# A hybrid encoder block on one core: the third head pair's row-sum loads behind the fourth pair's keys' copy in SP's queue

## The chip, the cores and the metric

The kernel runs on one core of a Trainium2 chip. TensorE (PE) multiplies matrices into PSUM, VectorE (DVE) and ScalarE (ACT) work elementwise, GpSimd (POOL) does little here but issue some DMAs, and SyncE (SP) issues nearly all the DMAs. The metric is the device time of one execution in microseconds (us), the median of several runs; less is better.

## The reference

One encoder layer over 512 positions of width 1024, in float32. Cut to what matters:

```python
h = rms_norm(x, attn_norm_g)
xr, gate, q, k, v = split(h @ w_in)
y_rnn  = (rg_lru(conv(xr), forward) + rg_lru(conv(xr), backward)) * gelu(gate)
y_attn = dilated_attention(q, k, v, rel_bias)     # 8 heads of 64
x = x + concat(rms_norm(y_rnn), rms_norm(y_attn)) @ w_out
x = x + square(relu(rms_norm(x) @ w_up)) @ w_down
return rms_norm(x, final_norm_g)
```

In the attention, each of eight heads has three dilated windows of keys with a relative bias, whose results are combined by their softmax sums. Together they amount to one softmax over the keys, with the logarithm of how often a key occurs added to its bias: `softmax(q k^T / 8 + bias) v`. A softmax row is divided by its sum; these row sums are one of the things that the change moves.

## The kernel before

**Matmuls in three.** Every large product is made of float32 numbers split into a high and a low part, and takes three matmuls (lines 312 to 314: high times high, high times low, low times high). ScalarE makes the high part of a weight block (whi, line 247), DVE the low part (wlo, line 269). The raw block arrives from DRAM in one of three buffers of 128 x 1024 floats (wraw); once DVE has made the low part, the buffer is free and SP loads the next block into it (`emit_dma`, line 230).

**Attention in pairs of heads.** The eight heads are four pairs, i = 0 to 3, written out as a loop over i and over four steps u of each pair (from line 1142 on). All positions are sorted by parity, 256 even ones and then 256 odd ones. For a pair, PE computes scores of four query tiles, each against 416 keys (`att_s`, line 805): two tiles use keys 0 to 511 as they stand, the other two need the first half of the keys once more behind the second. DVE writes the split keys into kk (line 784), and SP then copies their first half behind them inside SBUF, 256 KB (line 785, `s_lo`). Each group of six matmuls (two heads, three products) writes two PSUM tiles. DVE adds the bias and takes a row minimum (line 821), ScalarE takes the exponentials and adds up each row (line 822), PE transposes the result (line 841), and PE multiplies it with the values (`att_av`, line 941, tile pav).

**Row sums.** When a pair's exponentials are done, `att_z` (at u = 2) takes reciprocals of its row sums on DVE and SP writes them, transposed, to DRAM (zd, 16 KB, line 873). `att_zd` has SP read them back in two loads of 128 KB, spread over the partitions (zrow, line 878). DVE multiplies pav with zrow when it empties pav's PSUM bank (yp, line 947), which happens at the start of the next pair, just before DVE takes up that pair's scores.

**PSUM.** Score tiles, pav, and the output projection's tiles (pwo) share a pool of four banks that go round in turn ("pj"). The second head's tile of the fourth group of scores gets the bank that pav had.

**The output projection beside the fourth pair.** Work on W_out is woven into the pairs as fillers, three matmuls at a time. From the second half of the third pair on it is the product of the recurrent half (pwo). The attention half of W_out is multiplied by a scheme with sums of blocks. `load_x` starts it: SP loads the residual rows (x, eight loads of 256 KB, line 1045) and three raw blocks of W_out ("12", "22", "21" into ws, 512 KB each, line 1048), and DVE forms sums of them (lines 1051 to 1062). `load_x` puts these into a list `more`, of which one entry is run at the end of each step u.

**What sets the order of issues.** PE, ScalarE, DVE and POOL run in the order in which the code is written. So does SP within the loop over pairs, except that the loads of W_up blocks that are written behind the loop are put by a scheduler where a buffer becomes free. SP's queue is strictly in order: an issue that has to wait for a semaphore holds all behind it.

Of the kernel before, what the change touches and what calls it, by code (L numbers as in the profile page):

```python
# [98 lines left out]
def hybrid_kernel(ctx: ExitStack, tc, xw0, xw, xn, w_in, w_v, w_out, w_up, w_dn, gates, vecs, bias, fg, out):  # L99
# [118 lines left out]
    def oblock(b):  # L218
        return w_out[1, int(b[1]) - 1, int(b[0]) - 1]
# [578 lines left out]
    def att_s(p):  # L798
        for u in range(4):
            qt = QSEQ[u]  # L800
            w = {(0, 0): TH + TH - WN, (0, 1): 0, (1, 0): TH - WN, (1, 1): TH}[QT[qt]]
            pss = psq[p, u] = [ps_("ps", ("pj", "gs", "et", "pj")[u]) for _ in range(2)]
            for i, (a, b) in enumerate(((0, 0), (0, 1), (1, 0))):
                for e, r in enumerate(halves):
                    nc.tensor.matmul(pss[e][:, :NK], lhsT=qs_[p, a][r, P * qt:P * qt + P], rhs=kks[p][r, b, w:w + NK], start=i == 0, stop=i == 2)  # L805

    def att_e(p, u):
        qt = QSEQ[u]
        par, far = QT[qt]
        v = int(par != far)  # L810
        if u == 0:
            en[2 * p], en[2 * p + 1] = {}, {}
            zs[p] = small("zz", 8)
        pss = psq.pop((p, u))
        c0 = (WN + P) * far
        for e in range(2):
            h = 2 * p + e
            t = g_("e")
            mn = small("mn", 1)
            x = t[:, :NK] if far else t[:, S - NK:]  # L820
            nc.vector.tensor_tensor_reduce(x, pss[e][:, :NK], tws[h, v][:, c0:c0 + NK], 1.0, 3.0e38, OP.add, OP.min, mn)
            act(x, x, AF.Exp, scale=-1.0, bias=mn, accum_out=zs[p][:, 4 * e + qt:4 * e + qt + 1])
            en[h][qt] = t
            if u in (1, 3):
                del tws[h, v]
        if u == 3:
            del qs_[p, 0], qs_[p, 1], kks[p]
# [39 lines left out]
    def att_z(p):  # L867
        rz, zt = [work.tile([P, 32], FT, name=n, tag="zt", bufs=3) for n in ("rz", "zt")]
        z = zs.pop(p)
        nc.vector.reciprocal(rz.rearrange("p (e r q) -> p e r q", e=2, r=4),  # L870
                             bass.AP(tensor=z.tensor, offset=z.offset, ap=[z.ap[0], [4, 2], [0, 4], [1, 4]]))
        nc.vector.transpose(zt, rz)
        nc.sync.dma_start(bass.AP(tensor=zd.tensor, offset=zd.offset + 32 * P * p, ap=[[32, 4], [P, 32], [1, 32]]), zt)

    def att_zd(p):
        zrow[p] = g_("zrow")
        for e in range(2):
            nc.sync.dma_start(zrow[p][halves[e]], bass.AP(tensor=zd.tensor, offset=zd.offset + 32 * P * p + 4 * S * e, ap=[[0, 16], [S, 4], [1, S]]))

    def att_y(p):  # L880
        y_add(1)
# [50 lines left out]
    def att_av(p, jts):  # L932
        if 0 in jts:
            pav[p] = ps_("pav", "gs" if p == 3 else "pj")
        for jt in jts:
            parts = av_parts(jt)
            for i, (ci, co) in enumerate(parts):
                for e in range(2):
                    a = slice(64 * e, 64 * e + 64)
                    h = 2 * p + e  # L940
                    nc.tensor.matmul(pav[p][a, co], lhsT=vs[:, jt, h * DH:(h + 1) * DH], rhs=et[h, jt][:, ci],  # L941
                                     start=jt == 0 and i == 0, stop=jt == 3 and i == len(parts) - 1, skip_group_check=True)
            for e in range(2):
                del et[2 * p + e, jt]
        if 3 in jts:
            y = g_("yp")
            nc.vector.tensor_tensor(y[:, ::-1], pav.pop(p), zrow.pop(p), op=OP.mult)
            yat[p] = y
            if p == 3:
                att_a(p)  # L950
                att_q(p)

    def att_q(p):
        y_sq(yat[p], 1)

    def att_a(p):
        at[p] = g_("at")
        act(at[p], yat[p], AF.Copy, scale=vec("yg", 4 + p))
# [56 lines left out]
    def fill(n):  # L1015
        for _ in range(n):
            if fillers and fillers[0] is None:
                fillers.popleft()
                load_x()
            if fillers:  # L1020
                fillers.popleft()()
# [6 lines left out]
    more = deque()  # L1028

    def add_x():  # L1030
        for fn in more.popleft() if more else ():
            fn()

    def load_x():
        xb = big.tile([P, KD, S], FT, name="x1", tag="bigA")
        ws = big.tile([P, 4, 1024], FT, name="ws", tag="bigB")
        b12, b22, b21, s1 = [ws[:, i, :] for i in range(4)]
        tt = nc.vector.tensor_tensor

        def chunk(n, t):  # L1040
            raws[C_WA + OSEQ.index(n)] = t

        def x_in(g, n):
            x1[g, n] = xb[:, 2 * g + n, :]
            return lambda: nc.sync.dma_start(x1[g, n], xn[2 * g + n])

        def w_in(t, b):
            return lambda: nc.sync.dma_start(t, oblock(b))

        def sum1():  # L1050
            tt(s1, b12, raws[C_WA], op=OP.add)

        def sum2():
            t = work.tile([P, 1024], FT, name="tw", tag="tw", bufs=4)
            tt(t, s1, b22, op=OP.add)
            chunk("s2", t)
            t4 = work.tile([P, 1024], FT, name="tw", tag="tw", bufs=4)
            chunk("s4", t4)
            more[1].append(lambda: tt(t4, t, b21, op=OP.add))

        def sum3():
            tt(b12, b12, b22, op=OP.add)

        for n, t in (("s3", b12), ("22", b22), ("21", b21), ("s1", s1)):
            chunk(n, t)
        x_in(0, 0)()
        x_in(1, 0)()
        more.append([w_in(b12, "12")])
        more.append([w_in(b22, "22")])
        more.append([sum1, x_in(2, 0), x_in(3, 0), w_in(b21, "21")])  # L1070
        more.append([sum2, x_in(0, 1)])
        more.append([sum3, x_in(1, 1)])
        more.append([x_in(2, 1), x_in(3, 1)])
        more.append([emit_dma])
        more.append([emit_dma])
        more.append([emit_dma])
# [39 lines left out]
    def beside(*key):  # L1116
        for e in plan.pop(key, ()):
            e()
# [15 lines left out]
    def turn(p, jt):  # L1134
        for e in range(2):
            att_t(2 * p + e, jt)

    def corner(p, jt):
        for e in range(2):
            att_c(2 * p + e, jt)  # L1140

    with tc.manual_schedule(engines={nc.sync.engine}):
        for i in range(4):
            for u in range(4):
                beside(i, u, -1)
                if u == 0:
                    if i:
                        att_av(i - 1, range(4))
                    att_s(i)
                    att_e(i, 0)  # L1150
                    att_e(i, 1)
                if u > 1:
                    turn(i, 2 * u - 4)
                if u == 2:
                    att_z(i)
                beside(i, u, 0)
                fill(1)
                if u > 1:
                    corner(i, 2 * u - 4)
                if u == (2 if i == 2 else 3):  # L1160
                    att_zd(i)
                if (i, u) == (3, 2):
                    act(warm, epsb, AF.Sqrt)
                beside(i, u, 1)
                fill(1)
                if u == 0:
                    att_e(i, 2)
                    att_e(i, 3)
                if u == 1 and 1 <= i < 3:
                    att_q(i - 1)  # L1170
                    att_a(i - 1)
                if u > 1:
                    turn(i, 2 * u - 3)
                    corner(i, 2 * u - 3)
                if u < 2 and i < 3:
                    for e in range(2):
                        load_tw(2 * (i + 1) + e, 1 - u)
                beside(i, u, 2)
                fill(1)
                if u == 3 and 1 <= i < 3:  # L1180
                    att_y(i - 1)
                beside(i, u, 3)
                fill(1)
                add_x()
                beside(i, u, 4)
# [650 lines left out]
```

## Time and profile before

| | |
|---|---|
| three runs | 525.31, 527.17, 527.94 us; median 527.17 |
| profiled execution | 525.55 us, with a span of 523.7 us from the first to the last instruction |
| PE busy | 515.4 us (98% of the span) |
| PE weight loads busy | 443.7 us (85%) |
| DVE busy | 430.5 us (82%) |
| ScalarE busy | 351.6 us (67%) |
| DMA moved | 105.15 MB, 201 GB/s in the mean |
| granted TensorE clock | 1.000 |

The four attention pairs take the span from about 90 to 175 us; the change lies between 142 and 155 us. In the rows of the views, a timeline row has the start and the duration in us, the engine, the line, the operation, out<-in, how many instructions are merged in it, and in brackets the idle time before it with what ended it. The duration of an SP row is that of issuing the DMA; when its data has landed is told by "DMA to landing" (from issue to landing) in the view of a tile. A row of the list of waits has who waited <- for whom, the time in all, how often, and the longest. A row of a window has its length, the busy time and number of instructions of PE, PE's weight loads, DVE, ScalarE and POOL, the granted clock, the busy share of the DMA engines, and GB/s.

### The profile page before, as it was taken

The page shows a single profiled execution, that of the slowest core. Times are in us where ns is not written, and L with a number is a line of the kernel's source. Part 1 is how long each engine was busy: PE and PEld are TensorE (multiplying, and loading weights), DVE is VectorE, ACT ScalarE, POOL GpSimd, SP SyncE. Part 2 cuts the span into 40 slices and gives each one's busy share as a digit, 9 for nine tenths or more (in the row PEclk, how much of TensorE's full clock was granted, in tenths as well). Part 3 has the DMA queues.
Part 4 walks back from the last instruction along what each step waited for, and adds up shares of the span by engine and source line. Part 5 has one row for each costly group of instructions (what it writes and reads, how often), then busy time and mean ns, then how long its engine had stood idle before and what let it go on. Part 6 is the DMA issues. An engine that isn't in the chain of part 4 may idle for free.

```text
span 523.7 us, 8226 instructions
## 1 busy us (share of the span) xinstructions
PE 515.4 (98%) x3021; PEld 443.7 (85%) x3021; DVE 430.5 (82%) x667; ACT 351.6 (67%) x571; POOL 66.1 (13%) x89
## 2 busy tenths in 40 slices
PE   9999999999989999999999999999999999999995
PEld 7857888877768788899999888888999999888884
DVE  6898995877869898898779987889765977986985
ACT  7579946749747758585578665566567677665655
POOL 0182000000010221001300312001101300131000
PEclk9999999999999999999999999999999999999999
DMA  7736645456585699947595899976987496799804
GB/s 288 237 85 194 163 145 180 120 177 173 138 293 189 171 202 239 357 135 197 133 228 132 220 273 278 310 273 161 280 262 183 113 222 208 160 285 257 204 1 161
DMA packets 40329, 105.15 MB, mean 201 GB/s; under 512 B 5056, under 2 KB 13376, under 8 KB 40288
## 3 DMA queue, kind: packets, MB, share of 16 engines
q1 hardware_dynamic: 32448, 78.07, 44.7%
q0 software_dynamic: 7696, 26.32, 27.3%
q8 instruction: 24, 0.39, 0.3%
q10 hardware_dynamic: 144, 0.23, 0.1%
q14 instruction: 17, 0.14, 0.1%
HBM read 95.59 MB, written 4.29 MB: 191 GB/s over the span
## 4 chain that ended last, share of the span: by engine, by line
PE 96%; DMA 2%; DVE 0%; ACT 0%; issue 0%; SPq 0%; DVEq 0%
PE pu L314 10%; PE pu L313 10%; PE pu L312 10%; PE pd L313 10%; PE pd L314 10%; PE pd L312 10%; PE pqk L312 3%; PE pqk L314 3%; PE pqk L313 3%; PE pwo L312 2%; PE pwo L313 2%; PE pwo L314 2%; PE pav L941 2%; PE ps L805 2%; PE pt L841 2%; PE pp L312 1%
## 5 line engine op out<-in xcount | busy, mean ns | idle before, releaser
L269 DVE TENSOR_TENSOR wlo<-wraw,whi 128x1024 fp32r<-128x1024 f32 x71 | 86.5, 1219 | 22.3 <-ACT whi L247 22.1
L247 ACT ACTIVATE whi<-wraw 128x1024 fp32r<-128x1024 f32 x67 | 70.8, 1058 | 37.9 <-PE pd L314 17.0
L312 PE MATMUL pd<-whi,ah 128*128 128x512 f32 (+1 forms) x195 | 75.3, 386 | 0.0
L313 PE MATMUL pd<-wlo,ah 128*128 128x512 f32 (+1 forms) x195 | 75.3, 386 | 0.0
L314 PE MATMUL pd<-whi,al 128*128 128x512 f32 (+1 forms) x195 | 75.2, 386 | 0.0
L314 PE MATMUL pu<-hh,wlo 128*128 128x256 f32 x224 | 63.4, 283 | 0.0
L313 PE MATMUL pu<-hl,whi 128*128 128x256 f32 x224 | 63.4, 283 | 0.0
L312 PE MATMUL pu<-hh,whi 128*128 128x256 f32 x224 | 63.4, 283 | 0.0
L312 PE MATMUL pu<-h2h,whi 128*128 128x256 f32 (+1 forms) x200 | 60.1, 301 | 0.0
L314 PE MATMUL pu<-h2h,wlo 128*128 128x256 f32 (+1 forms) x200 | 60.1, 300 | 0.0
L313 PE MATMUL pu<-h2l,whi 128*128 128x256 f32 (+1 forms) x200 | 60.0, 300 | 0.0
L269 DVE TENSOR_TENSOR wlo<-tw,whi 128x1024 fp32r<-128x1024 f32 x37 | 45.2, 1222 | 17.1 <-ACT whi L247 17.1
L247 ACT ACTIVATE whi<-tw 128x1024 fp32r<-128x1024 f32 x38 | 40.1, 1058 | 24.6 <-PE pd L314 6.1
L313 PEld LDWEIGHTS pu<-hl,whi 128*128 128x128 f32 x224 | 43.0, 192 | 0.0
L312 PEld LDWEIGHTS pu<-hh,whi 128*128 128x128 f32 x224 | 43.0, 192 | 0.0
L314 PEld LDWEIGHTS pu<-hh,wlo 128*128 128x128 f32 x224 | 43.0, 192 | 0.0
L312 PEld LDWEIGHTS pd<-whi,ah 128*128 128x128 f32 x195 | 36.6, 188 | 7.4
L314 PEld LDWEIGHTS pd<-whi,al 128*128 128x128 f32 x195 | 36.6, 188 | 7.3
L313 PEld LDWEIGHTS pd<-wlo,ah 128*128 128x128 f32 x195 | 36.6, 188 | 7.3
L247 ACT ACTIVATE whi<-ts 128x1024 fp32r<-128x1024 f32 x24 | 25.4, 1060 | 25.6 <-PE pd L314 17.8
L312 PEld LDWEIGHTS pu<-h2h,whi 128*128 128x128 f32 x200 | 38.3, 191 | 1.3
L313 PEld LDWEIGHTS pu<-h2l,whi 128*128 128x128 f32 x200 | 38.3, 191 | 1.3
(283 smaller groups left out, 1221.3 us busy)
## 6 DMA issues: line engine op xcount, KB each, us to landing
wraw<-in_w_up_dram SPq DMA_DIRECT2D x25, 512.0 KB, 4.1
ts<-in_w_dn_dram POOLq DMA_DIRECT2D x24, 512.0 KB, 13.2
wraw<-in_w_dn_dram SPq DMA_DIRECT2D x24, 512.0 KB, 10.3
tw<-in_w_up_dram SPq DMA_DIRECT2D x15, 512.0 KB, 6.9
tw<-in_w_up_dram POOLq DMA_DIRECT2D x15, 512.0 KB, 8.3
wraw<-in_w_in_dram SPq DMA_DIRECT2D x13, 512.0 KB, 3.6
ts<-in_w_dn_dram SPq DMA_DIRECT2D x8, 512.0 KB, 8.7
tw<-in_w_dn_dram SPq DMA_DIRECT2D x8, 512.0 KB, 4.8
```

Source lines behind the costliest of these rows:

```text
L247: act(hi, raws[i], AF.Copy)
L269: nc.vector.tensor_tensor(lo, r, f(splits[i][0]), op=OP.subtract)
L312: nc.tensor.matmul(o, lhsT=a[0], rhs=b[0], start=bool(first), stop=False, skip_group_check=on)
L313: nc.tensor.matmul(o, lhsT=a[0], rhs=b[1], start=False, stop=False, skip_group_check=on)
L314: nc.tensor.matmul(o, lhsT=a[1], rhs=b[0], start=False, stop=bool(last), skip_group_check=on)
L805: nc.tensor.matmul(pss[e][:, :NK], lhsT=qs_[p, a][r, P * qt:P * qt + P], rhs=kks[p][r, b, w:w + NK], start=i == 0, stop=i == 2)
L841: nc.tensor.transpose(pt[:, i * P:(i + 1) * P], en[h][qt][:, k:k + P], ident)
L941: nc.tensor.matmul(pav[p][a, co], lhsT=vs[:, jt, h * DH:(h + 1) * DH], rhs=et[h, jt][:, ci], start=jt == 0 and i == 0, stop=jt == 3 and i ...
```

## The change

Two edits, both to what SP issues in the third pair (i = 2). `att_zd(2)`, the two loads of the third pair's row sums, moves from step u = 2 to step u = 3, where the other pairs have it; there it stands behind the step's first work, which for the third pair holds the copy of the fourth pair's keys. And the first W_out block ("12"), which was loaded at the end of step u = 2, is loaded at the end of u = 3 together with the second ("22").

```diff
@@ load_x
         x_in(0, 0)()
         x_in(1, 0)()
-        more.append([w_in(b12, "12")])
-        more.append([w_in(b22, "22")])
+        more.append([])
+        more.append([w_in(b12, "12"), w_in(b22, "22")])
         more.append([sum1, x_in(2, 0), x_in(3, 0), w_in(b21, "21")])
@@ the loop over pairs i and steps u
                 beside(i, u, 0)
                 fill(1)
                 if u > 1:
                     corner(i, 2 * u - 4)
-                if u == (2 if i == 2 else 3):
+                if u == 3:
                     att_zd(i)
```

This is SP's queue in the third pair, steps u = 2 and u = 3, as the difference between the kernels. zrow are the row-sum loads, ws the W_out blocks, wraw a W_up block, kk the keys' copy, x the residual rows. A name in brackets is a counter that the issue waits for: the DMAHW ones count completed DMAs (eight of them, used in turn), the others instructions of an engine.

```order
 L1045 DMA x_1608<-in_xn_dram 128x512 [waits DMAHW0_49,PE_49]
 L1045 DMA x_1608<-in_xn_dram 128x512 [waits DMAHW1_49]
-L878 DMA zrow<-zd 64x1x512 [waits DMAHW7_49,DMAHW2_49]
-L878 DMA zrow<-zd 64x1x512 [waits DMAHW3_49]
-L1048 DMA ws<-in_w_out_dram 128x1024 [waits DMAHW4_49]
-L230 DMA wraw<-in_w_up_dram 128x1024 [waits DMAHW5_49,DVE_49]
-L785 DMA kk<-kk 128x2x256 [waits DMAHW6_49,DVE_49]
+L230 DMA wraw<-in_w_up_dram 128x1024 [waits DMAHW2_49,DVE_49]
+L785 DMA kk<-kk 128x2x256 [waits DMAHW3_49,DVE_49]
+L878 DMA zrow<-zd 64x1x512 [waits DMAHW7_49,DMAHW4_49]
+L878 DMA zrow<-zd 64x1x512 [waits DMAHW5_49]
+L1048 DMA ws<-in_w_out_dram 128x1024 [waits DMAHW6_49]
```

The two row-sum loads and the first W_out block, which stood ahead of the W_up block and the copy, now stand behind them. The loads still wait for the counter of the row sums' write to DRAM (DMAHW7); the copy waits for DVE alone.

This is PE in the changed kernel, in the fourth pair's scores, from the second group of six matmuls on. (The order of PE's instructions is the same in both.)

```order
L805 MATMUL ps<-kk,qh 128x416 x4
L805 MATMUL ps<-kk,ql 128x416 x2
L805 MATMUL ps<-kk,qh 128x416 [waits DMAHW3_49,PE_49]
L805 MATMUL ps<-kk,qh 128x416 [waits PE_49]
L805 MATMUL ps<-kk,qh 128x416 x2
L805 MATMUL ps<-kk,ql 128x416 x2
L805 MATMUL ps<-kk,qh 128x416 [waits DVE_49] x2
```

The third group's first matmul waits for the copy; it did so before, with another counter. The fourth group waits for DVE to have emptied its banks.

This is DVE's product that empties pav of the third pair:

```order
-L947 TENSOR_TENSOR yp<-pav,zrow 128x512 [waits DMAHW3_49,DMAHW2_49,PE_49]
+L947 TENSOR_TENSOR yp<-pav,zrow 128x512 [waits DMAHW5_49,DMAHW4_49,PE_49]
 L821 ISA e,mn<-ps,tw 128x416 [waits DMAHW7_49,DMAHW6_49,PE_49]
 L821 ISA mn 128x1
```

It stays where it was, in front of DVE's work on the fourth pair's scores, and waits for the two row-sum loads at their new place.

## The prediction

> **What bounds the kernel now.** I first read the page's busy times and the shares of the chain that ended last.
>
> ```profile
> PE 515.4 (98%) x3021; PEld 443.7 (85%) x3021; DVE 430.5 (82%) x667; ACT 351.6 (67%) x571; POOL 66.1 (13%) x89
> PE 96%; DMA 2%; DVE 0%; ACT 0%; issue 0%; SPq 0%; DVEq 0%
> ```
>
> TensorE sets the end: it is busy 98% of the span. The program's matmuls are not changed, so the only thing that this change can win or lose is time in which PE stands still. The second view is the list of PE's own waits over the whole span:
>
> ```profile
> PE ps L805 <- DMA kk<-kk: 2.1, 1, 2.1
> PE pwarm L142 <- PEq L1825: 0.8, 1, 0.8
> ```
>
> There are two rows, and the second is the start of the program. The first is one wait, for a DMA that copies a pair's key halves inside SBUF (kk<-kk). Third, the timeline of PE shows where. The first two rows are the third pair's scores and the matmul behind them, the others those of the fourth pair.
>
> ```profile
> 133.35 0.65 PE L805 MATMUL ps<-kk,qh 64*128 64x416 f32 x4
> 134.58 0.56 PE L805 MATMUL ps<-kk,qh 64*128 64x416 f32 x4
> 135.14 0.56 PE L805 MATMUL ps<-kk,qh 64*128 64x416 f32 x4
> 135.82 0.50 PE L312 MATMUL pqk<-h_hi,whi 128*128 128x512 f32 x1
> ...
> 152.61 0.65 PE L805 MATMUL ps<-kk,qh 64*128 64x416 f32 x4
> 156.08 0.65 PE L805 MATMUL ps<-kk,qh 64*128 64x416 f32 x4 [2.08 <-DMA kk<-kk]
> 157.40 0.51 PE L312 MATMUL pwo<-whi,yh 128*128 128x512 f32 x1
> ```
>
> A pair's scores are four groups of six matmuls. The first two use keys as DVE wrote them; the third and fourth read the copied half. In the third pair the four groups take 135.82 - 133.35 = 2.47 us, in the fourth 157.40 - 152.61 = 4.79 us. The difference of 2.32 us is what the late copy costs. It is a little more than the 2.08 us of the named wait, because the matmul stream also has to start again.
>
> Fourth, why the copy is late. These are SP's issues around it, its wait in this stretch, and the DVE rows that release them:
>
> ```profile
> 142.83 0.59 SPq L873 DMA_DIRECT2D zd<-zt  x1
> 143.51 1.19 SPq L1045 DMA_DIRECT2D x<-in_xn_dram  x2
> 148.62 1.18 SPq L878 DMA_DIRECT2D zrow<-zd  x2
> 149.85 0.57 SPq L1048 DMA_DIRECT2D ws<-in_w_out_dram  x1
> 150.52 0.38 SPq L230 DMA_DIRECT2D wraw<-in_w_up_dram  x1
> 151.00 0.65 SPq L785 DMA_DIRECT2D kk<-kk  x1
> SPq L878 <- DMA zd<-zt: 4.6, 2, 3.9
> 146.17 1.22 DVE L269 TENSOR_TENSOR wlo<-wraw,whi 128x1024 fp32r<-128x1024 f32 x1
> 147.31 0.69 DVE L784 TENSOR_TENSOR kk<-kraw,kk 128x512 fp32r<-128x512 f32 x1
> ```
>
> SP issues strictly in its order. It stood 3.9 us, from 144.70 to 148.62, in front of the third pair's row-sum loads (zrow<-zd), because the row sums had not yet landed in DRAM (zd<-zt, issued at 142.83). What the copy itself needs, the DVE subtraction at line 784, was done at 148.00. The copy went out at 151.00, 3.0 us later, only because of what stood ahead of it. It then moved behind 1.25 MB:
>
> ```profile
> 151.00 4.95 DMA kk<-kk
> DMA to landing us min/median/max: 2.5/2.6/5.0
> DMA to landing us min/median/max: 2.4/2.6/3.2
> ```
>
> The first row is from the chain of waits; the second gives all four pairs' copies, the third all eight row-sum loads, from issue to landing. The other three pairs' copies, with no large load right ahead, took about 2.6 us.
>
> **The change part by part.** No instruction is added or removed; five issues of SP change places.
>
> *The copy.* In its new place it is behind the two x loads and one W_up block (wraw). That block needs the buffer that line 269 frees at 146.17 + 1.22 = 147.39; its issue takes 0.38, so SP is free again at about 147.8. The copy then goes out when line 784 is done, at about 148.1: 2.9 us earlier. Landing is bounded by 2.5 us (an undisturbed copy) and 5.0 us (this one, with 1.25 MB ahead; now it is 0.5 MB and the rest of the x loads), so it lands between 150.6 and 153.1. PE wants it for the third group, at 152.61 + (134.58 - 133.35) = 153.84. Both ends are in time, by 0.7 us at the worst, so the wait goes wholly: **-2.32 us**. It would come back only with a landing of over 5.7 us.
>
> *The row sums.* They still can't go before zd has landed at about 148.6. They follow the copy's 0.65 us of issue and go at 148.75 and 149.35, only 0.13 us later than before. But they now have 0.75 MB ahead of them. Their reader is the DVE product yp<-pav,zrow, with what follows it:
>
> ```profile
> 152.75 0.69 DVE L947 TENSOR_TENSOR yp<-pav,zrow 128x512 f32<-128x512 f32 x1 [2.13 <-PE pav L941]
> 156.93 0.59 DVE L821 CUSTOM_DVE_ANT_0 e<-ps,tw 128x416 f32<-128x416 f32 x1 [1.32 <-PE ps L805]
> 158.98 1.22 DVE L1051 TENSOR_TENSOR ws<-ws,wraw 128x1024 f32<-128x1024 f32 x1
> 171.43 0.42 DVE L902 TENSOR_TENSOR ol<-at,oh 128x256 fp32r<-128x256 f32 x1 [1.28 <-ACT oh L897]
> DMA to landing us min/median/max: 4.7/4.7/4.7
> 143.51 5.58 DMA x<-in_xn_dram
> ```
>
> The last two rows are landings behind a full queue: the W_up block of 150.52 with 0.75 MB ahead (4.7 us, for its own 0.5 MB), and the first x load. So the second row-sum load lands between 149.35 + 2.5 = 151.85 and 149.35 + 5.6 = 154.95. I take 3.3 us: the block's 4.7 us less the 0.375 MB that a row-sum load is smaller, at the 288 GB/s that the queue moved from 150 to 154 us, which is the mean of these rows:
>
> ```profile
> 150.00:152.00 2.00, 2.00 (x22) 1.41 (x20) 0.62 (x1) 0.00 (x0) 0.00 (x0) 1.00 0.84 280
> 152.00:154.00 2.00, 2.00 (x16) 1.05 (x12) 1.22 (x4) 0.00 (x0) 0.00 (x0) 1.00 0.85 297
> 160.00:162.00 2.00, 2.00 (x10) 1.65 (x10) 1.72 (x3) 0.95 (x4) 0.00 (x0) 1.00 0.00 0
> ```
>
> That is 152.65, just before DVE starts yp today: **0**. The cover is the 2.13 us for which DVE waits on pav there. Gone, it costs this: yp frees the PSUM bank that the fourth group's second head writes, so PE loses time once yp ends after 152.61 + (135.14 - 133.35) = 154.40, that is once the sums land after 153.71. At 4.7 us of landing it is 0.34 us, at 5.6 us it is 1.24.
>
> *W_out's first block* goes out at about 150.0 instead of 149.85, the second at 150.6 instead of 151.7, the x loads and the third block about 1.1 us earlier. The reader of the first is DVE's sum at line 1051, now at 158.98. DVE loses its 1.32 us of idleness at 156.93 and gets there at 157.66, 7.6 us after the issue; a landing as late as the slowest of these blocks holds that sum, not PE: **0**. If that cover is gone too, DVE's 1.28 us of idleness at 171.43 takes up what it is late.
>
> *What is late next.* From 157.40 on PE has no wait in the whole list, so nothing new appears as long as its suppliers come 2.3 us earlier with it. The nearest is ScalarE's exponentials for the transposes:
>
> ```profile
> 163.00 0.82 PE L841 MATMUL pt<-ident,e 128*128 128x128 f32 x6
> 159.99 0.19 ACT L822 ACTIVATION_READ_ACCUMULATOR e<-e,mn 128x1 f32 x1
> 157.56 0.64 ACT L822 ACTIVATE e<-e,mn 128x416 f32<-128x416 f32 x1 [0.78 <-DVE mn L821]
> SPq L230 <- DVE wlo L269: 144.0, 41, 11.3
> ```
>
> They end at 160.18, and 0.78 us of that is a gap that the stall made, so they end at 159.4; the transposes move to 160.7, 1.3 us behind. The DMA rings are empty from 160 us (share 0.00 above), so no backlog is carried on. Later weight blocks are issued when DVE has split an earlier one (the last row: 41 times), so they are paced by the work and come earlier with it: **0**.
>
> Sum: -2.32 us. The profiled execution took 525.55 us (span 523.7), so it would take 523.2. It stands 1.6 us below the median of the three runs (527.17) and 0.24 above their lowest. From the median the same sum gives **524.9 us**.
>
> **The rivals.**
>
> *The row sums become the wait.* For it: they change from an empty queue to one with 0.75 MB ahead, and the rows with such a queue took 4.7 to 5.6 us. Against: they are small. With 5.6 us PE loses 1.24 us again and the gain is 1.1: 526.1 us. [...]
>
> *The copy isn't early: the change doesn't do what it says.* The chain of waits names the DVE product at line 982, not line 269, as what came before the W_up block's issue:
>
> ```profile
> 149.88 0.75 DVE x L982
> 150.63 0.27 SPq L230
> ```
>
> If the block really waited for that, it would still go at 150.6 and hold the copy till 151.0, as today. With 0.5 MB ahead instead of 1.25 the copy would land in time or nearly, but the row sums would go at 151.7 and 152.3 and, with the same 3.3 us, land at 155.6. yp would end at 156.3, PE's fourth group would start then and not at 156.73 as today, and the gain would be 0.4 us: 526.8. Against: SP's issues at 149.85 and 150.52 follow each other without a pause, and the buffer's last reader is line 269.
>
> *The gain is given back later.* 2.3 us is less than DVE's or a DMA chain's slack may be somewhere in the 360 us that follow; DVE is 82% busy. Against: PE's list of waits has no row there. No change: 527.2.
>
> *More than the sum.* The profiled execution is one of the quick ones. If the other runs are slower because this very copy is later in them, the change takes that too: 527.17 - 525.55 = 1.6 more, 523.3. Nothing in one trace tells.
>
> *Slower: the row sums so late that they cost more than the copy did.* PE's fourth group would have to start after 156.73, where it starts today; that is decided once the sums land after 156.0, 6.7 us after their issue. The slowest W_out block of this stretch took 8.7:
>
> ```profile
> 156.73 0.56 PE L805 MATMUL ps<-kk,qh 64*128 64x416 f32 x4
> DMA to landing us min/median/max: 5.3/7.0/8.7
> ```
>
> With 8.7 they land at 158.05, yp ends at 158.74, and PE is 2.0 us later than today: 529.2. Against: a block is four times as large as a row-sum load.
>
> **How the numbers follow.** Forecast 54%, row sums 12%, copy not early 7%, given back 11%, more 12%, slower 4%. A measurement of this kernel tells about 0.5%, 2.64 us, from no change. The forecast of 2.3 us lies just inside that bound; with medians of runs that spread over 2.6 us I give it four chances in nine to come out beyond, 24%, and with the 12% of "more" faster is 0.36. Slower by more than that is most of the last rival: 0.03. The rest, 0.61, is within. The range goes from 522.8 (the lowest run less the sum, and a little) to 527.3 (no gain).
>
> **What would show it.** In the profile after: PE's list of waits without the row of kk<-kk; 2.5 us from the fourth pair's first score matmul to the pwo matmul behind it; SP's copy at about 148.1, ahead of the row sums at 148.8; yp at line 947 still released by PE pav and not by a DMA. If yp is released by zrow, the first rival holds; if SP's W_up block still goes at 150.6, the second; if a new PE wait of 1 to 2 us stands after 160 us, the third. A trace that has all the steps right and a time that hasn't moved would make the prediction wrong in its last step only.

## The result

The changed kernel took 524.34 us in the median of nine executions, the kernel before 527.40 us: a ratio of 0.995 with a 95% interval of 0.9929 to 0.9971. Three of all executions stand outside every comparison, because TensorE was much slower in them than in the others: the profiled one of the changed kernel (1044.51 us; its large matmuls took 670 ns in the mean instead of 386, though its granted clock is listed as 1.000), one of the kernel before (735.14, mean granted clock 0.656) and one of an experiment (861.35, 0.558). The profile shown here is from a repetition of the changed kernel (first experiment below), whose profiled execution took 523.33 us with a span of 521.5.

The page's busy times and PE's list of waits, of the changed kernel:

```profile
PE 515.0 (99%) x3021; PEld 443.6 (85%) x3021; DVE 430.1 (82%) x667; ACT 351.1 (67%) x571; POOL 66.2 (13%) x89
PE pwarm L142 <- PEq L1825: 0.8, 1, 0.8
PE pxr L453 <- ACT w3h L357: 0.2, 1, 0.2
```

The wait for kk<-kk is gone, and nothing has come in its place; both rows are from the first 5 us of the program. SP's issues, PE's fourth score groups and DVE's reader of the row sums, from the timeline of the changed kernel:

```profile
143.02 0.59 SPq L873 DMA_DIRECT2D zd<-zt  x1
143.70 1.28 SPq L1045 DMA_DIRECT2D x<-in_xn_dram  x2
147.60 0.33 SPq L230 DMA_DIRECT2D wraw<-in_w_up_dram  x1
148.21 0.65 SPq L785 DMA_DIRECT2D kk<-kk  x1
148.95 1.20 SPq L878 DMA_DIRECT2D zrow<-zd  x2
150.21 1.08 SPq L1048 DMA_DIRECT2D ws<-in_w_out_dram  x2
...
152.80 0.65 PE L805 MATMUL ps<-kk,qh 64*128 64x416 f32 x4
154.03 0.55 PE L805 MATMUL ps<-kk,qh 64*128 64x416 f32 x4
154.59 0.56 PE L805 MATMUL ps<-kk,qh 64*128 64x416 f32 x4
155.26 0.50 PE L312 MATMUL pwo<-whi,yh 128*128 128x512 f32 x1
...
153.72 0.69 DVE L947 TENSOR_TENSOR yp<-pav,zrow 128x512 f32<-128x512 f32 x1 [2.56 <-PE ps L805]
DMA to landing us min/median/max: 4.0/4.0/4.0
```

The copy goes at 148.21 instead of 151.00, right after DVE has made the keys. The four score groups take 155.26 - 152.80 = 2.46 us, as in the third pair, instead of the 4.79 of before. But yp starts 0.9 us after the first score matmul, though pav is done by then: it now waits for the row sums, whose second load went at about 149.6 and took 4.0 us (last row, issue to landing). The bracket of the yp row names PE's score matmuls, whose results yp doesn't read; in a later profile of the same kernel (last experiment) it names the load:

```profile
153.86 0.69 DVE L947 TENSOR_TENSOR yp<-pav,zrow 128x512 f32<-128x512 f32 x1 [2.43 <-DMA zrow<-zd]
```

PE does not notice: neither profile has a wait for yp.

### The profile page after: what moved, and what is told of

Same layout as the page of the kernel before. It is cut to its first block, busy times and chain, and to the rows that moved or that the text cites. A ratio compares the mean times of both kernels' runs of the same rounds, so it can differ in the third digit from the quotient of the medians.

```text
span 1042.7 us, 8224 instructions
## 1 busy us (share of the span) xinstructions
PE 1036.4 (99%) x3021; PEld 754.3 (72%) x3021; DVE 441.6 (42%) x667; ACT 356.6 (34%) x571; POOL 61.4 (6%) x89
## 4 chain that ended last, share of the span: by engine, by line
PE 99%; ACT 0%; DVE 0%; issue 0%
PE pu L313 10%; PE pu L314 10%; PE pu L312 10%; PE pd L312 10%; PE pd L313 10%; PE pd L314 10%; PE pqk L312 3%; PE pqk L313 3%; PE pqk L314 3%; PE pwo L314 3%; PE pwo L313 3%; PE pwo L312 3%; PE pav L941 2%; PE pt L841 2%; PE ps L805 2%; PE pg L528 1%
## 5 line engine op out<-in xcount | busy, mean ns | idle before, releaser
L312 PE MATMUL pd<-whi,ah 128*128 128x512 f32 (+1 forms) x195 | 130.6, 670 | 0.0
L313 PE MATMUL pd<-wlo,ah 128*128 128x512 f32 (+1 forms) x195 | 130.6, 670 | 0.0
L314 PE MATMUL pd<-whi,al 128*128 128x512 f32 (+1 forms) x195 | 130.3, 668 | 0.0
L313 PE MATMUL pu<-hl,whi 128*128 128x256 f32 x224 | 99.0, 442 | 0.0
L314 PE MATMUL pu<-h2h,wlo 128*128 128x256 f32 (+1 forms) x200 | 95.9, 480 | 0.0
L312 PE MATMUL pu<-h2h,whi 128*128 128x256 f32 (+1 forms) x200 | 95.7, 478 | 0.0
L314 PEld LDWEIGHTS pu<-hh,wlo 128*128 128x128 f32 x224 | 79.1, 353 | 0.0
L313 PEld LDWEIGHTS pu<-hl,whi 128*128 128x128 f32 x224 | 78.3, 349 | 0.2 <-issue 0.2
L312 PEld LDWEIGHTS pu<-hh,whi 128*128 128x128 f32 x224 | 77.7, 347 | 0.2 <-issue 0.2
L314 PEld LDWEIGHTS pu<-h2h,wlo 128*128 128x128 f32 x200 | 67.1, 336 | 5.2 <-issue 4.8
```

Of the source, the lines that this page charges most:

```text
L312: nc.tensor.matmul(o, lhsT=a[0], rhs=b[0], start=bool(first), stop=False, skip_group_check=on)
L313: nc.tensor.matmul(o, lhsT=a[0], rhs=b[1], start=False, stop=False, skip_group_check=on)
L314: nc.tensor.matmul(o, lhsT=a[1], rhs=b[0], start=False, stop=bool(last), skip_group_check=on)
```

## The experiments

All were timed against the kernel before on the same chip. This table splits each profiled span at two marks of PE: the fourth pair's first score matmul, and the first pwo matmul behind the scores. The last two columns are PE's named wait in the scores, in this one profiled execution, and how many of all executions had a mean granted clock of 0.996 or less. (For the kernel before these are its executions beside all the experiments; the row of the copy issued by ScalarE takes two runs together.)

| kernel | to the scores | scores | to the end | PE's wait | low clock |
|---|---|---|---|---|---|
| before | 152.61 | 4.79 | 366.3 | 2.08, kk | 36 of 79 |
| before, second profile | 152.84 | 4.40 | 367.9 | 1.68, kk | (among them) |
| changed | 152.80 | 2.46 | 366.2 | none | 0 of 30 |
| only the row sums moved | 152.57 | 3.68 | 366.2 | 0.58, yp | 0 of 12 |
| only the W_out block moved | 153.37 | 3.01 | 366.2 | 0.28, kk | 0 of 11 |
| row sums behind all | 153.58 | 6.43 | 367.8 | 3.52, yp | 7 of 7 |
| copy issued by ScalarE | 152.73 | 2.47 | 366.2 | none | 1 of 18 |
| copy behind all | 152.86 | 8.05 | 368.1 | 4.27, kk | 6 of 6 |

### The changed kernel again

No edit.

> The changed kernel once more, unchanged, because its one profile so far shows PE at about half its speed for the whole run (PE busy 1036.4 us) and can't be read against the profile of before. Theory (the late keys' copy was the only PE wait, and it goes): the copy is issued near 148.1 us and lands before 153.8; PE's list of waits has no kk<-kk row; from the fourth pair's first score matmul to the pwo matmul behind it 2.5 us instead of 4.79; yp at line 947 still follows PE pav; span 521.2 to 522.5; 2.3 to 3.0 us faster than the kernel before. First rival (row sums become the wait): yp is released by a DMA, and up to 1.2 us of PE wait stands in the fourth score group. Second rival (the copy isn't early): the W_up block is still issued near 150.6.

Measured: 523.93 against 526.25 us, ratio 0.9951 (0.9931 to 0.9971). The first theory holds in all but one point: yp no longer follows PE pav. That is the first rival's sign, but its PE wait isn't there. The second rival falls: the W_up block went at 147.60.

### The kernel before again

No edit.

> The kernel before once more, unchanged, for a second profile of it and as a measure of what no change looks like. Its nine runs spread over 4.2 us (524.83 to 529.01), those of the changed kernel over 1.1 us (523.95 to 525.00). Theory with the rival of more gain than the sum: the extra time of the longer runs is the same copy landing still later, so in this profile the PE wait for kk<-kk differs from 2.08 us by about as much as the run's time differs from 525.55, within 0.5 us. Against it: the wait is again 2.1 us within 0.3 while the time is another, so the spread comes from elsewhere. Timed: a ratio of 1.000 within 0.002.

Measured: 527.18 us, ratio 1.0007 (0.9979 to 1.0034). The profiled execution took 526.91 us, 1.36 more than the first one, and yet its wait for the copy is shorter. The list of waits, the copy's issue, the landing of all four pairs' copies, and a table of stretches of 2 us (the third last column is the granted clock):

```profile
PE ps L805 <- DMA kk<-kk: 1.7, 1, 1.7
149.63 0.65 SPq L785 DMA_DIRECT2D kk<-kk  x1
DMA to landing us min/median/max: 2.5/2.6/6.1
154.00:156.00 2.00, 0.33 (x6) 0.12 (x3) 1.84 (x8) 1.60 (x5) 0.00 (x0) 1.00 1.03 409
156.00:158.00 2.00, 2.00 (x14) 1.62 (x15) 1.25 (x5) 1.62 (x6) 0.00 (x0) 0.82 1.03 405
158.00:160.00 2.00, 2.00 (x7) 1.52 (x6) 2.00 (x5) 2.00 (x9) 0.00 (x0) 0.50 0.40 146
160.00:162.00 2.00, 2.00 (x9) 1.63 (x8) 0.13 (x2) 0.61 (x1) 0.00 (x0) 0.82 0.00 0
162.00:164.00 2.00, 2.00 (x11) 1.64 (x10) 2.00 (x3) 0.73 (x1) 0.00 (x0) 1.00 0.00 0
```

So this longer execution is not one in which the copy landed still later; that reading falls. The copy even went 1.37 us earlier than in the first profile, but, with the same 1.25 MB ahead, took 6.1 us to land instead of 4.95, so the wait is only 0.4 us shorter: the time of issue alone doesn't set it. What comes instead is in the clock. Behind the wait, TensorE is granted half its clock (0.50 from 158 to 160 us). The clock lacks 0.36 + 1.00 + 0.36 = 1.72 us of these 6, which is 3.4 us at one half. The first profile of the kernel before, and that of the changed kernel, have 1.00 in this whole stretch. From the first pwo matmul to the first transpose behind it PE took 164.43 - 157.24 = 7.19 us, against 163.00 - 157.40 = 5.60 in the first profile: the drop cost 1.6 us.

```profile
157.24 0.78 PE L312 MATMUL pwo<-whi,yh 128*128 128x512 f32 x1
164.43 0.82 PE L841 MATMUL pt<-ident,e 128*128 128x128 f32 x6
```

The other executions have no profile, but their mean clocks and times go together. The 43 executions of the kernel before with a mean clock above 0.996 have a median of 525.55 us, its 36 others one of 527.94. Seven of the 36 stand apart, with 0.991 and a median of 529.78; no profile shows why.

### One half: only the row sums move

```diff
-                if u == (2 if i == 2 else 3):
+                if u == 3:
                     att_zd(i)
```

> One half of the change: only the third pair's row-sum loads move behind the keys' copy; the first W_out block stays ahead, at the end of step u = 2, and is issued near 144.8 us because SP no longer stands there for the row sums. Theory (SP's wait in front of the row-sum loads, not the W_out block's bytes, made the copy late): the copy goes at about 148.1 with 1 MB ahead, lands 152 to 153.1, before PE's third group at 153.84: the whole gain, within 0.5 us of the changed kernel. Rival (bytes ahead count as much): the copy lands after 153.84 and PE keeps a wait of 0.5 to 1.5 us.

Measured: 524.58 us, ratio 0.9970 (0.9955 to 0.9986), 0.65 us more than the changed kernel. That is just outside the 0.5 us of the theory. The copy was in time or nearly, as the theory has it (PE's list has no wait for it, and the third group came 1.37 us behind the first, against 1.23 in the changed kernel): SP's wait in front of the row-sum loads (3.9 us in the first profile of the kernel before) had made it late. But the gain isn't whole, for a reason that neither theory named. PE's list of waits, PE's fourth group and yp:

```profile
PE ps L805 <- DVE yp L947: 0.6, 1, 0.6
155.50 0.64 PE L805 MATMUL ps<-kk,qh 64*128 64x416 f32 x3 [0.58 <-DVE yp L947]
154.75 0.69 DVE L947 TENSOR_TENSOR yp<-pav,zrow 128x512 f32<-128x512 f32 x1 [4.27 <-PE ps L805]
DMA to landing us min/median/max: 5.3/5.5/5.7
```

With the W_out block ahead as well, the two row-sum loads took 5.3 and 5.7 us to land (last row), yp ended at 155.4, and the fourth group's second head had to wait for it. Moving the W_out block too takes this wait away.

### The other half: only the W_out block moves

```diff
-        more.append([w_in(b12, "12")])
-        more.append([w_in(b22, "22")])
+        more.append([])
+        more.append([w_in(b12, "12"), w_in(b22, "22")])
```

> The other half: only the first W_out block moves behind the copy; the row-sum loads stay in front and hold SP until the row sums have landed, at about 148.6. Theory: the copy goes at about 150.3 with 0.75 MB ahead and lands 154.2 to 155.0, so a PE wait of 0.4 to 1.2 us for kk<-kk is left, and the gain is 1.1 to 1.9 us. Rival (bytes ahead count, not SP's wait): the wait is gone and the whole gain of 2.3 us is there. Rival (neither half does anything alone): no gain.

Measured: 524.50 us, ratio 0.9970 (0.9955 to 0.9986).

```profile
149.06 1.18 SPq L878 DMA_DIRECT2D zrow<-zd  x2
150.96 0.64 SPq L785 DMA_DIRECT2D kk<-kk  x1
155.05 0.65 PE L805 MATMUL ps<-kk,qh 64*128 64x416 f32 x4 [0.28 <-DMA kk<-kk]
DMA to landing us min/median/max: 3.9/3.9/3.9
```

Counted back from the first score matmul, the copy goes 153.37 - 150.96 = 2.41 us ahead instead of 152.61 - 151.00 = 1.61, and with 0.5 MB less ahead of it it landed in 3.9 us instead of 4.95 (last row). Together that is 1.85 us, and a wait of 0.28 us is left, less than the 0.4 to 1.2 that was expected. So taking away the block's issue and bytes removes most of the wait, just as taking away SP's stand for the row sums did in the other half: either cure is nearly enough for the copy. Each half is worth some 1.7 us, and the two together not the sum, since there is only one wait to remove.

### The row sums further back

The changed kernel, with the row-sum loads behind both W_out blocks.

```diff
-                if u == 3:
+                if u == 3 and i != 2:
                     att_zd(i)
...
                 add_x()
+                if (i, u) == (2, 3):
+                    att_zd(i)
```

> The changed kernel, but the third pair's row-sum loads go still further back, behind both W_out blocks: 1.75 MB ahead of them instead of 0.75. Theory (yp frees the PSUM bank of the fourth score group, so row sums that land after about 153.8 cost PE one for one): they landed 4.0 us after issue with 0.75 MB ahead; with 1 MB more at 290 to 380 GB/s they land at about 156.4 to 157.2, yp ends near 157.5, and PE waits 2.3 to 3.2 us in the fourth group for yp: the gain is gone, 526 to 527.5 without a drop of the clock. Rival (DVE's idleness hides it): no PE wait, the time of the changed kernel, 523.9.

Measured: 529.54 us, ratio 1.0050 (1.0021 to 1.0079): slower than the kernel before.

```profile
PE ps L805 <- DVE yp L947: 3.5, 1, 3.5
158.50 0.69 DVE L947 TENSOR_TENSOR yp<-pav,zrow 128x512 f32<-128x512 f32 x1 [6.48 <-DMA zrow<-zd]
159.25 0.46 PE L805 MATMUL ps<-kk,qh 64*128 64x416 f32 x2 [3.52 <-DVE yp L947]
160.00:162.00 2.00, 2.00 (x7) 1.55 (x7) 2.00 (x9) 2.00 (x7) 0.00 (x0) 0.61 0.07 23
162.00:164.00 2.00, 2.00 (x7) 1.57 (x6) 2.00 (x7) 2.00 (x7) 0.00 (x0) 0.53 0.00 0
```

The theory's chain is there: late row sums, late yp, PE's fourth group waiting for the PSUM bank. The size expected was too small (3.52 us came, not 2.3 to 3.2), and here too the clock falls to one half behind the wait, for (0.78 + 0.94) / 0.5 = 3.4 us. All seven executions have a mean clock of 0.995 or less.

### The copy from another queue

The kernel before, with the fourth pair's copy issued by ScalarE.

```diff
-            nc.sync.dma_start(f(k[:, :, S:]), f(k[:, :, :TH]))
+            (nc.scalar if p == 3 else nc.sync).dma_start(f(k[:, :, S:]), f(k[:, :, :TH]))
```

> The kernel before with one thing changed: the fourth pair's keys' copy is issued from ScalarE's queue instead of SP's, so it waits for DVE's subtraction alone while the row-sum loads stay in front in SP's queue (the W_up block then falls behind the W_out blocks in SP's queue). Theory (only the place in SP's queue made the copy late): it goes near 148.2, lands by 151.5, PE has no wait for kk<-kk nor for yp, and the time is that of the changed kernel within 0.5 us, 523.4 to 524.4. Rival (the gain of the change comes from the W_out and x loads that go earlier with it): these stay where they were, so no gain, 526 to 527.

Measured: 523.48 us, ratio 0.9947 (0.9925 to 0.9969). The whole gain, with the row sums where they were before.

```profile
148.89 0.68 ACTq L785 DMA_DIRECT2D kk<-kk  x1
148.84 1.18 SPq L878 DMA_DIRECT2D zrow<-zd  x2
152.73 0.65 PE L805 MATMUL ps<-kk,qh 64*128 64x416 f32 x4
155.20 0.50 PE L312 MATMUL pwo<-whi,yh 128*128 128x512 f32 x1
```

Only the copy's place mattered for the wait: the row sums and the first W_out block kept theirs in SP's queue, and the score groups take 2.47 us. The rival isn't tested as cleanly as was meant, because with the copy and the W_up block out of their way the second W_out block and the x loads went earlier here too (x at 151.19 instead of 152.34). Against it stands that PE's list of before has no wait for any of these loads, and that the span behind the scores is the same in both kernels, 366.2 and 366.3 us. One of the 18 executions of this version has the lower mean clock (0.994, 527.42 us); it has no profile, so its cause is open.

### The wait made longer

The kernel before, with the copy behind all three W_out blocks.

```diff
-            nc.sync.dma_start(f(k[:, :, S:]), f(k[:, :, :TH]))
+            if p < 3:
+                nc.sync.dma_start(f(k[:, :, S:]), f(k[:, :, :TH]))
...
-        more.append([w_in(b22, "22")])
-        more.append([sum1, x_in(2, 0), x_in(3, 0), w_in(b21, "21")])
+        more.append([w_in(b22, "22"), w_in(b21, "21")])
+        more.append([sum1, x_in(2, 0), x_in(3, 0)])
...
                 add_x()
+                if (i, u) == (2, 3):
+                    nc.sync.dma_start(f(kks[3][:, :, S:]), f(kks[3][:, :, :TH]))
```

> The kernel before with its one PE wait made about twice as long: the keys' copy goes behind all three W_out blocks (1.75 MB ahead, issued near 151.8). The last profile of the kernel before showed the granted clock at one half for some 3.3 us right behind the wait, 1.6 us lost, and the profile of the first did not. Theory (the wait itself may drop the clock, and the longer it is the more often): PE wait 3.3 to 4.3 us; nearly every execution has a mean clock of 0.996 or less; time 529 to 531, that is the wait's extra 1.7 and a drop in nearly all runs. Rival (the drop comes from elsewhere and has nothing to do with the wait): the same share of runs at a low clock as the kernel before has (20 of 45), and 527.5 to 528.5.

Measured: 530.40 us, ratio 1.0068 (1.0043 to 1.0092). (Line 805 is line 806 here.)

```profile
PE ps L806 <- DMA kk<-kk: 4.3, 1, 4.3
156.00:158.00 2.00, 0.00 (x0) 0.00 (x0) 0.00 (x0) 1.03 (x4) 0.00 (x0) 1.00 1.05 394
158.00:160.00 2.00, 1.47 (x8) 1.50 (x10) 0.06 (x1) 0.00 (x0) 0.00 (x0) 0.50 1.04 403
160.00:162.00 2.00, 2.00 (x9) 1.31 (x8) 2.00 (x7) 1.43 (x5) 0.00 (x0) 0.50 0.15 57
162.00:164.00 2.00, 2.00 (x6) 1.58 (x5) 1.23 (x3) 1.79 (x5) 0.00 (x0) 0.50 0.00 0
164.00:166.00 2.00, 2.00 (x8) 1.60 (x7) 0.22 (x1) 0.00 (x0) 0.00 (x0) 0.80 0.00 0
```

A wait of 4.27 us, twice the one of before, came with half clock for (1.0 + 1.0 + 1.0 + 0.4) / 0.5 = 6.8 us, and all six executions are at 0.994 or less: wait, clocks and time are as the theory has them. In the row-sum experiment, with a wait of 3.52 us for another thing, all seven are at 0.995 or less, and where the profiles have waits of 0.28 and 0.58 us, for either thing, none of 23 executions has the lower clock. So in these runs the drop went with the length of PE's wait, not with its cause.

Length isn't all. Stretches of 0.2 us show when the clock changes, here in the second profile of the kernel before, behind the wait and again behind the program's last matmul:

```profile
157.20:157.40 0.20, 0.20 (x3) 0.16 (x2) 0.20 (x3) 0.01 (x1) 0.00 (x0) 0.72 0.88 348
160.60:160.80 0.20, 0.20 (x2) 0.15 (x2) 0.00 (x0) 0.01 (x1) 0.00 (x0) 0.74 0.00 0
522.40:522.60 0.20, 0.00 (x0) 0.00 (x0) 0.00 (x0) 0.00 (x0) 0.00 (x0) 0.79 1.07 361
```

A mean of 0.72 between 1.00 and 0.50 puts the fall at 157.29 us; in the same way the rise is at 160.70, 3.41 us later, and the second fall at 522.52. In the row-sum experiment the two falls are at 160.46 and 525.68, in this one at 157.99 and 526.63. The distances between the two falls are 365.23, 365.22 and 368.64 us; the last is longer than the others by about one stretch of 3.41 us. 365.23 / 3.41 is close to 107; with 365.23 / 107 = 3.413 us the distances are 107, 107 and 108 times the same length, and the stretches at half clock are one, one and two times that. From this I estimate that the clock changes at the ends of windows of 3.413 us that don't start with the wait; the fit to these three profiles is all that speaks for it. Counted back on this estimate from the fall at the end of the first profile of the kernel before (523.30, from a mean of 0.75 between 523.20 and 523.40), such ends lie at 154.66 and 158.07: they cut its wait, 154.00 to 156.08, into 0.66 and 1.42 us, and the clock stayed at 1.00. In the second profile the whole wait of 1.68 us lies in one window, 153.88 to 157.29, and the clock fell at its end. If the estimate holds, this tells why much the same wait lowers the clock in one execution and not in another. How much idleness in a window is enough isn't shown: 1.68 us went with a fall there, while 1.69 us behind the last matmul of the first profile (518.20 to the window's end at 519.89) did not.

### The two best beside each other

> The changed kernel beside the copy-on-ScalarE kernel on the same chip, because the two were timed in different calls (523.93 and 523.48 us). Both have no PE wait in their profiles, so both theories say equal: 523.3 to 524.3, within 0.5 us of each other, and in neither a mean clock below 0.996 in more than one execution of twelve.

> The copy issued by ScalarE, beside the changed kernel. Theory (PE without a wait is the floor of this place): equal to the changed kernel within 0.5 us. Rival (the changed kernel's row sums land so close to their limit, 153.7, that some of its executions wait): this one is faster by 0.5 to 1 us in the median.

Measured: the changed kernel 523.88 us (ratio 0.9947, 0.9926 to 0.9969), the copy on ScalarE 523.21 (0.9938, 0.9917 to 0.9958). The medians differ by 0.67 us, which is outside the 0.5 us of the theory and inside the 0.5 to 1 us of the rival: five of the six executions with the copy on ScalarE are at 523.34 us or less, and two of the ten of the changed kernel. The rival's mechanism isn't seen in the two profiles. Neither has a PE wait in the scores, from the first score matmul on both take 2.48 + 366.2 us, and the 0.6 us between them is there at about 33 us already, where both kernels are the same. So the ScalarE version may be better by some tenths; whether row sums that are late in some executions make the difference stays open.

## Why the prediction was right

The forecast was 524.9 us, 2.3 less than before; measured were 524.34 and a difference of 3.06 us in the first comparison, 2.3 in both later ones. The mechanism, a late copy as PE's only wait, was right; that the medians differ by just this number is partly luck, as *more than the sum* below says. Point by point:

- **The copy.** Forecast: issued at about 148.1 and the wait wholly gone, -2.32 us. Measured: 148.21, and the score groups fell from 4.79 to 2.46 us, -2.33. The reading of the whole cost from the score groups, not from the named wait of 2.08, was right.
- **The row sums.** The place was right (issued at 148.95), the size was a little short: 3.3 us to landing was taken, the second load took 4.0 in the first profile and 3.4 in the later one. yp therefore was led by the row sums and not by pav, against what was to show the step right. It cost PE nothing, as the forecast had it, but with little to spare: in the first profile yp ended at 153.72 + 0.69 = 154.41 and the fourth group came at 154.59, 0.2 us later; in the later one 0.8 us were left. The half experiment went past the limit (PE wait 0.58), the last-place one far past it (3.52).
- **The W_out block.** DVE's sum at line 1051 was forecast for 157.66 and came at 158.41, because DVE was held at yp. It held nobody.
- **What is late next.** The exponentials were to end 1.3 us ahead of the transposes. They ended at 160.13 against 160.83, 0.7 us ahead, again through yp. Still covered.
- **Nothing given back.** From the first pwo matmul to the end the span is 366.3 us before and 366.2 after. That rival falls.
- **The copy isn't early.** Falls: the W_up block went at 147.60, when line 269's buffer was free; the chain's naming of line 982 was no dependence.
- **More than the sum.** This rival's time came partly true and its reason was wrong. It took the longer executions of the kernel before for ones with a longer wait for the copy. The second profile of before has a shorter one, and a clock at one half behind it. 36 of 79 executions of before have the lower mean clock, none of 30 of the changed kernel, so the change takes off the wait (2.33 us in the score groups of the first profiles) and, in nearly half of the executions, a drop of the clock on top. That is the term the sum lacked: it priced the wait by its length alone, with the mean clock of one execution in which it hadn't dropped. The median of before is therefore one of a mixture. Against the 524.04 us of the changed kernel's 30 executions, the 36 of before with the lower clock are 3.9 us longer in the median and the other 43 only 1.5, less than the 2.3 of the sum. Where these 0.8 us are lost no run here shows; the wait differs between executions (2.08 and 1.68 us in two profiles), and the changed kernel's own spread from 523.21 to 525.16.
- **The slower side.** The mechanism is real, as the row sums behind all blocks show (529.54 us, a dropped clock included); the changed order stays short of it.

## What to carry to other kernels

A stall of TensorE can cost more than its own length, as it did here: in the kernel with a wait of 2.08 and 1.68 us in its two profiles 36 of 79 executions had a lower mean clock, and in the one profiled of them 3.4 us at a clock of 0.50 cost 1.6 us more; in the two kernels with waits of 0.28 and 0.58 us none of 23 executions had the lower clock. If executions of one kernel spread where another's don't, look at the granted clock in short windows behind each stall, in more than one profile. And when an issue is moved forward in a DMA queue that goes in order, as SP's did here (the copy's keys were ready at 148.00 us and it went at 151.00, behind row-sum loads in front of which SP had stood 3.9 us), work out how late what it passes may become: here neither move alone gave the whole gain, since the copy needed less ahead of it and the row sums had to stay inside their cover, of which 0.2 us was left in one profile and 0.8 in another.

## What the runs showed of the hardware

The granted clock fell to 0.50 with PE waits of 1.68, 3.52 and 4.27 us, and stayed there for 3.4, 3.4 and 6.8 us; with a wait of 2.08 us in another execution it did not fall. The falls came 1.4 and 1.2 us behind the end of the first two waits and 0.5 us before the end of the third, and 365.23, 365.22 and 368.64 us ahead of the fall at the end of the program. In the two kernels whose profiles have waits of 3.52 and 4.27 us all 13 executions had a lower mean clock, in the two with 0.28 and 0.58 none of 23. Landing times in SP's queue grew in these profiles with what had been issued just ahead: for a row-sum load 2.5 us with none of these blocks ahead, 3.4 and 4.0 behind 0.75 MB in two profiles, 5.3 and 5.7 behind 1.25 MB, 6.8 behind 1.75 MB. They aren't fixed by it: the keys' copy took 4.95 us in one execution and 6.1 in another behind the same 1.25 MB.
